# Another order of a hybrid-layer step: planner costs, sample search and first feed-forward units

## Chip, cores and metric

The kernel runs on one core of a Trainium2 chip. The metric is the device time of one execution in microseconds (us). Of the engines, TensorE (PE) multiplies, VectorE (DVE), ScalarE (ACT) and GpSimd (POOL) work elementwise, and SyncE (SP) issues most DMAs.

## What is computed

One step of one decoder layer, for a prompt of 1024 tokens and for 64 sample tokens (8 sequences of 8, each with 4096 past positions in a paged cache). The two token mixers run on the same input; cut to what matters here:

```python
def select_keys(scores, q_pos, topk):            # topk = 256
    scores = jnp.where(admissible, scores, -jnp.inf)
    _, idx = lax.top_k(scores, topk)
...
def token_mixer(x, ...):
    z = split_projection(x @ w_in)
    attn = attend(q_a, k_a, v_a, q_i, k_i, z['w_i'])     # softmax over the selected keys
    log_a = jax.nn.log_sigmoid(z['a_b'] @ w_alpha2 + b_alpha) / GATE_TAU
    o_b, s_new = gla_chunked(q_b, k_b, v_b, log_a, s0, chunk)   # 4 heads, chunks of 64
    o_b = rms_norm(o_b) * gla_norm_g * jax.nn.silu(z['g_b'])
    merged = jax.nn.sigmoid(z['gate_a']) * (attn @ w_attn_o) + jax.nn.sigmoid(z['gate_b']) * (o_b @ w_gla_o)
    return merged @ w_out, ...
...
def residual_block(x, mix_out, ...):
    h = layer_norm(DN_ALPHA * x + mix_out, ln1_g, ln1_b)
    ff = jnp.square(jax.nn.relu(h @ w_ff1)) @ w_ff2      # 1024 -> 4096 -> 1024
    return layer_norm(DN_ALPHA * h + ff, ln2_g, ln2_b)
```

## The kernel before

The 1088 tokens lie on the free axis in three chunks of 384, 384 and 320 columns (the third holds the sample tokens), and features on the partitions. Every large product is done three times with operands split in a high and a low part (`xh`·`wh`, `xl`·`wh`, `xh`·`wl`); a weight tile is loaded as `wr`, ACT rounds it to `wh`, and DVE or POOL subtracts to get `wl` (`sub` picks the one that the planner's clock has free first; in the feed-forward part the tiles are `w`).

Nothing schedules itself on the chip: every engine runs its instructions in the order of the program. That order is made by a planner in Python. `Clock` holds a time for each engine, adds a cost for each instruction (`cost`), and knows when each tile is ready. Work is written as generators (`Stream`), which yield the tiles that they need next. `Order.run` takes the first stream in its list whose needs are ready by PE's time plus 0.2, and records its next piece; where none is, the one that is ready soonest. Each stream has a `slack` (how far it may run ahead of DVE and ACT) and a `margin`. All recording goes through one line (223), so that the profile shows that line everywhere, and the rows are told apart by tiles.

In the first half (`front`) the streams are, among others:
- `top_prompt`: the threshold of the 256 largest index scores of each prompt token, found bit by bit in 32 rounds; DVE counts (`jk`) in two groups of tiles (`ga`, `gb`), each with small steps `_m`, `_u`, `_f`. Its masks `msk` are needed by the attention.
- `top_sample`: the same for the sample tokens, with the counts on ACT (`jka`, two per round), a small product that sums pairs of partitions on PE (`ppr`), and small steps on DVE (`gs_m`, `gs_u`, `gs_f`), 33 rounds in all. It may start at job `merge_at + SEARCH`.
- `heads`: the four heads of the gated linear attention. For head h, DVE scans the log gates (`cu`), multiplies `gk` by their exponential, and then PE starts with `psas` from `gq` and `gk`.
- `main`: the projections as a list of jobs, among them 16 `gate` jobs that serve as filler, `pmb` (o_b @ w_gla_o), `pma` (attn @ w_attn_o) and `pwo` (merged @ w_out).
- `at_soft` and `at_pv`: prompt attention: scores `psq`, masked `pp`, transpose `ppt`, split `phl`, values `pov`. It starts when the heads and `top_prompt` are done.
- `ob_load`: loads the gated output of the heads back from DRAM as `obl` and splits it into `obh` and `obl` for `pmb`. It may start three jobs ahead of the merge when the last `pov` is done, and else with the merge.

In the second half (`back`) the norms (`ln`: products `plm`, `plv`, `plr`, tiles `h`) feed the feed-forward units (`ff1_unit`: product `pf`, relu, square, split into `a`), with the attention of the sample tokens between (`psc`, `pob`, `sa`, `pso`).

Of the kernel before, what the change touches and what calls it, by code (L numbers as in the profile page):

```python
# [17 lines left out]
AF = mybir.ActivationFunctionType  # L18
# [5 lines left out]
P = 128  # L24
# [11 lines left out]
CH = ((0, 384), (384, 384), (768, 320))  # L36
# [9 lines left out]
NBW = 5  # L46
NCW = 8
NSM = 6
NSH = 6
# [9 lines left out]
GAHEAD = 2  # L59
BLEAD = 1  # L60
MARGIN = 0.0
DMAL = 2.75
LAG = 0.3
LAGS = {"pe": 0.2}
POOLLAG = 0.4
M_IP = 0.0
M_IS = 0.0
M_TS = 0.3
SEARCH = -22
M_GL = 0.0  # L70
# [3 lines left out]
M_SC = 1.0  # L74
M_SD = 0.5
WLATE = 4.0

# [5 lines left out]
def view(ap, offset, dims):  # L83
    return bass.AP(tensor=ap.tensor, offset=ap.offset + offset, ap=[list(d) for d in dims])


class Clock:
# [3 lines left out]
    def __init__(self, uses):  # L91
        self.uses, self.left, self.seen, self.key = uses, {}, {}, {}
        self.free, self.owed, self.short = {}, {}, []
        self.t = dict.fromkeys(("pe", "dve", "act", "pool", "sp"), 0.0)
        self.ring = {}
        self.fly = deque(maxlen=8)
        self.written = {}
        self.used = {}
        self.after = {}
        self.banks = [None] * 8  # L100
        self.psum = set()
        self.pinned = set()
# [58 lines left out]
    def cost(self, e, op, outs, ins):  # L161
        n = outs[0].free_size() if callable(outs[0].free_size) else outs[0].free_size
        aps = len(outs) + len(ins)
        if e == "pe":
            dt = ins[-1].dtype
            f = 4 if dt == F32 and op != "transpose" or dt == F32R and n < 256 else 1
            return max(f * n / 2400 + 0.0135, 0.11)
        if e == "dve":
            return 0.069 + n * (0.00625 if op == "reciprocal" else 0.00104) + 0.06 * (aps > 3)
        if e == "act" and "dma" in op:  # L170
            return 0.06
        if e == "act":
            return (0.051 if any(x.tensor.name in self.psum for x in ins) else 0.093) + n / 1200 + 0.093 * (aps - 2)
        if e == "pool":
            if "dma" in op:
                return 1.25
            if op == "tensor_scalar":
                return 0.26 + 0.00333 * n
            return 0.13 + n * 0.0009 if op in ("affine_select", "memset") else 0.15 + n * 0.0021
        return 0.52 if hasattr(outs[0].tensor, "tag") else 0.7  # L180

    def note(self, e, op, a, k):
# [9 lines left out]
        if e == "sp" and len(self.fly) == 8:  # L192
            self.t[e] = max(self.t[e], self.fly[0])
        start = max([self.t[e]] + [self.ready(x) for x in ins] + [self.after.get(x.tensor.name, 0.0) for x in outs])
        self.t[e] = end = start + self.cost(e, op, outs, ins)
        if "dma" in op:
# [93 lines left out]
def hybrid_step(ctx, tc, A, O, uses):  # L290
# [43 lines left out]
    with ExitStack() as ph:  # L334
        back(ph, tc, env, A, O)
    return {k: n for k, n in clock.seen.items() if k[1] is not None}


def front(ph, tc, env, A, O):
# [1108 lines left out]
    for h in range(4):  # L1448
# [8 lines left out]
    more_gates(4)  # L1457
    for j in range(2):
# [58 lines left out]
    mix_at = len(jobs)  # L1517
    env["deep"] = mix_at - 2
    env["alone"] = (merge_at,)
# [112 lines left out]
    s_gl = order.add(heads(), margin=M_GL)  # L1632
    s_ts = order.add(top_sample(), slack=1.0, margin=M_TS)
    s_main = order.add(main(), engines=())
# [8 lines left out]
def back(ph, tc, env, A, O):  # L1643
# [114 lines left out]
    def ln(c, z, s, gi, emit, tag):  # L1758
# [46 lines left out]
        normed.add((tag, c))  # L1805

    def add(s, z, f):

# [18 lines left out]
    def outputs(c, get, make):  # L1827
# [10 lines left out]
        for f in range(8):  # L1838
# [11 lines left out]
            if f < 7 or c < 2:  # L1850
                add(s[:, :n], z, f)
        order.add(ln(c, z, s[:, :n], 0, emit_h(c), 1), at=0)

# [3 lines left out]
    def project():  # L1857
# [4 lines left out]
        for f in range(8):  # L1862
# [3 lines left out]
            mg[f, 1] = (st[:, 0], st[:, 1])  # L1866
        order.add(ln(0, zs, env["rsum"], 0, emit_h(0), 1), at=0)
        yield from outputs(1, lambda f: W.get(f, 2, NRW), page)
# [248 lines left out]


    def ff1_unit(w, f, c, a):
        n = CH[c][1]  # L2120
        ps = bank("pf1", True)
        yield from mm3(ps[:, :n], w, [hc[k, c] for k in range(8)])
        unpin(ps)
        r = small("fr")
        act.activation(r[:, :n], ps[:, :n], AF.Relu)
# [59 lines left out]
    def feed():  # L2185
        for i0, (cc, k0, np_) in zip(first, plan):
            a, z, s = {}, {c: [] for c in cc}, {}
            if k0 == 0:
                ws = {}
                for c in cc:  # L2190
                    yield lambda: (1, c) in normed
                    for f in range(np_ + 8):
# [20 lines left out]
            for f in range(8):  # L2213
                w = W.get(i0 + np_ + f, *((2, NRW) if cc == (2,) else ()))
                for c in cc:
                    n = CH[c][1]
                    z[c].append((yield from ff2_unit(w, f, c, a, np_, False)))
                    if k0 + np_ == 32:
# [4 lines left out]
                        if f == 7:  # L2223
                            order.add(ln(c, z[c], s[c][:, :n], 2, emit_y(c), 2), at=0)

# [60 lines left out]
def build(arrays, uses):  # L2286
    nc = bacc.Bacc("TRN2", target_bir_lowering=False, num_devices=1, dynamic_dma_scratch_size=SCRATCH)
    A = {k: nc.dram_tensor(k, v.shape, mybir.dt.from_np(v.dtype), kind="ExternalInput").ap() for k, v in arrays.items()}
    O = {k: nc.dram_tensor(k, s, F32, kind="ExternalOutput").ap() for k, s in OUT.items()}
    with tile.TileContext(nc) as tc:  # L2290
        return nc, hybrid_step(tc, A, O, uses)

# [20 lines left out]
```

## Time and profile before

| | us |
|---|---|
| median of 3 runs | 2145.94 (2145.61 to 2147.4) |
| profiled execution | 2150.88 |
| its span (first to last instruction) | 2149.2 |
| PE busy | 2061.4 (96%) |
| weight loads of PE busy | 1965.4 (91%) |
| DVE busy | 1347.3 (63%) |
| ACT busy | 1030.8 (48%) |
| POOL busy | 717.0 (33%) |

The span is the time between the first and the last instruction of the profiled execution. The granted TensorE clock is 0.983 of full on the mean. A row of waits says which engine's instruction waited for which other one's; a wait for several is put down to the one that came last.

### The profile page before, as it was taken

What the parts mean: (1) busy time and instruction counts of PE and PEld (TensorE: products, weight loads), DVE (VectorE), ACT (ScalarE), POOL (GpSimd) and SP (SyncE); (2) the same over time, 40 slices, a digit from 0 to 9 for tenths busy, and PEclk for the clock granted to TensorE, in tenths of its full rate; (3) what the DMA queues carried; (4) which work ended last, traced back from release to release, by engine and by line L of the source; (5) the groups of instructions that cost most, each with busy time, mean ns of one, the idle gap of its engine ahead of it and who ended that gap; (6) DMA issues with size and microseconds to landing.
All of it is one profiled execution on the core that took longest, in us unless ns stands there. A gap on an engine that the chain in (4) does not pass through costs nothing.

```text
span 2149.2 us, 34662 instructions
## 1 busy us (share of the span) xinstructions
PE 2061.4 (96%) x12492; PEld 1965.4 (91%) x12507; DVE 1347.3 (63%) x2806; ACT 1030.8 (48%) x2010; POOL 717.0 (33%) x543
## 2 busy tenths in 40 slices
PE   7999988998999999998999999999999999999997
PEld 7978977897989999998998999989999999999996
DVE  7887998898236666532656854665654446367635
ACT  5665234444667667776133424445453333245543
POOL 5144211215121121231334335545544333343342
PEclk9999998999999999999999999999999999999998
DMA  9363401211213242344393224545433442145442
GB/s 334 150 181 109 143 29 42 64 59 48 75 48 126 72 128 71 93 174 143 129 344 112 79 76 118 163 126 157 142 94 113 147 134 72 61 129 169 169 148 83
DMA packets 182860, 260.79 MB, mean 121 GB/s; under 512 B 21392, under 2 KB 118672, under 8 KB 182688
## 3 DMA queue, kind: packets, MB, share of 16 engines
q1 hardware_dynamic: 175136, 233.14, 33.4%
q0 software_dynamic: 7552, 25.43, 3.7%
q8 instruction: 98, 1.61, 0.3%
q14 instruction: 74, 0.61, 0.1%
HBM read 209.00 MB, written 49.51 MB: 120 GB/s over the span
## 4 chain that ended last, share of the span: by engine, by line
PE 69%; DVE 17%; issue 5%; ACT 4%; DMA 2%; POOL 2%; SPq 0%; DVEq 0%; ACTq 0%; POOLq 0%
PE pf L223 30%; PE gate L223 8%; DVE jk L223 5%; PE pwo L223 3%; PE psc L223 2%; PE psv L223 2%; PE po L223 2%; PE pmb L223 2%; PE gb L223 2%; PE qi L223 1%; PE pob L223 1%; PE psq L223 1%; PE pov L223 1%; PE ppt L223 1%; PE psi L223 1%
## 5 line engine op out<-in xcount | busy, mean ns | idle before, releaser
L223 PE MATMUL pf<-a,w 128*128 128x384 f32 (+1 forms) x2304 | 401.7, 330 | 3.9 <-ACT a L223 1.9
L223 PE MATMUL pf<-h,w 128*128 128x384 f32 (+1 forms) x2304 | 396.2, 329 | 2.2 <-DVE h L223 2.2
L223 PEld LDWEIGHTS pf<-a,w 128*128 128x128 f32 x2304 | 380.3, 189 | 6.4 <-ACT a L223 2.5
L223 PEld LDWEIGHTS pf<-h,w 128*128 128x128 f32 x2304 | 380.2, 189 | 4.8 <-DVE h L223 3.1
L223 POOL TENSOR_TENSOR wl<-wr,wh 128x1024 fp32r<-128x1024 f32 (+1 forms) x68 | 156.1, 2300 | 546.4 <-ACT wh L223 450.3
L223 DVE TENSOR_TENSOR w<-wr,w 128x512 fp32r<-128x512 f32 x190 | 178.8, 966 | 74.0 <-ACT w L223 72.6
L223 ACT ACTIVATE w<-wr 128x512 fp32r<-128x512 f32 x272 | 156.8, 619 | 49.1 <-PE pf L223 26.4
L223 POOL TENSOR_TENSOR a<-fr,a 128x384 fp32r<-128x384 f32 (+1 forms) x79 | 76.0, 963 | 275.1 <-ACT a L223 267.5
L223 POOL TENSOR_TENSOR w<-wr,w 128x512 fp32r<-128x512 f32 x82 | 113.0, 1390 | 81.7 <-ACT w L223 76.0
L223 PE MATMUL gate<-xh,wh 128*128 128x384 f32 (+1 forms) x384 | 130.2, 339 | 0.0
L223 DVE TENSOR_TENSOR acc<-acc,pf 128x384 f32<-128x384 f32 (+1 forms) x136 | 72.5, 538 | 87.1 <-PE pf L223 85.1
L223 PE MATMUL gate<-xl,wh 128*128 128x384 f32 (+1 forms) x384 | 126.1, 328 | 0.0
L223 PE MATMUL gate<-xh,wl 128*128 128x384 f32 (+1 forms) x384 | 126.0, 328 | 0.0
L223 ACT ACTIVATE fr<-pf 128x384 f32<-128x384 f32 (+1 forms) x96 | 45.1, 470 | 154.2 <-PE pf L223 153.5
L223 DVE TENSOR_TENSOR fr<-fr,pf 128x384 f32<-128x384 f32 (+1 forms) x96 | 50.8, 529 | 101.7 <-ACT fr L223 100.6
L223 ACT ACTIVATE wh<-wr 128x1024 fp32r<-128x1024 f32 (+1 forms) x75 | 74.4, 1006 | 56.6 <-PE pmb L223 35.2
L223 ACT ACTIVATE a<-fr 128x384 fp32r<-128x384 f32 (+1 forms) x96 | 48.8, 508 | 95.1 <-DVE fr L223 93.9
L223 DVE TENSOR_SCALAR_CACHE_REDUCE jk<-sc,gb_f 128x896 int8<-128x896 f32 (+2 forms) x96 | 92.7, 966 | 1.1
L223 DVE TENSOR_SCALAR_CACHE_REDUCE jk<-sc,ga_f 128x1024 int8<-128x1024 f32 (+2 forms) x96 | 88.4, 921 | 1.0
L223 PE MATMUL psv<-wh,xh 128*128 128x256 f32 (+1 forms) x288 | 83.0, 288 | 0.0
L223 PE MATMUL psv<-wh,xl 128*128 128x256 f32 (+1 forms) x288 | 81.3, 282 | 0.0
L223 PE MATMUL psv<-wl,xh 128*128 128x256 f32 (+1 forms) x288 | 81.3, 282 | 0.0
(460 smaller groups left out, 5116.7 us busy)
## 6 DMA issues: line engine op xcount, KB each, us to landing
wr<-wff SPq DMA_DIRECT2D x256, 256.0 KB
wr<-w SPq DMA_DIRECT2D x43, 512.0 KB
ckr<-kT SPq DMA_DIRECT2D x256, 64.0 KB
ga_s<-gate SPq DMA_DIRECT2D x16, 544.0 KB
ci_s<-cig SPq DMA_DIRECT2D x16, 512.0 KB
kir<-ci_s SPq DMA_DIRECT2D x16, 512.0 KB
wr<-wout SPq DMA_DIRECT2D x13, 512.0 KB
mgp<-ga_s SPq DMA_DIRECT2D x16, 384.0 KB
```

What stands on the lines that cost most here:

```text
L223: r = f(*a, **k)
```

## The change

It has three parts.

The planner's numbers: `Clock` now keeps the last spans of DVE and POOL that use the port which the two share (`locks`), and starts an instruction of one behind such a span of the other; it adds 1.28 where ACT's function table changes; a scan costs 0.0021 per element instead of 0.00104, a POOL instruction 0.175 + 0.0022 n instead of 0.15 + 0.0021 n, and the 40% that were added to a POOL result's readiness (`POOLLAG`) are dropped.

The sample search: it may start eight jobs earlier (`SEARCH` −22 to −30), with a slack of 3.0 instead of 1.0 and a margin of 0.2 instead of 0.3.

The back: a norm is put into the list of streams behind the norms that are still under way, not ahead of them. The first four feed-forward units of a chunk, which waited for the whole norm (`(1, c) in normed`), are computed by `ff1_first`: for each of the first six k-tiles, as the norm emits it, the products of all four units, then the last two k-tiles unit by unit. (The `Counted` exception ends a first counting pass early and leaves the instructions alone; `NGATE` and `DEEP` name numbers that were there.)

```diff
-POOLLAG = 0.4
+POOLLAG = 0.0
-M_TS = 0.3
-SEARCH = -22
+M_TS = 0.2
+SEARCH = -30
...
+    def locks(self, e, op, outs, ins):
+        n = outs[0].free_size() if callable(outs[0].free_size) else outs[0].free_size
+        if e == "pool":
+            return "dma" not in op and op not in ("iota", "memset")
+        if any(x.tensor.name in self.psum for x in outs + ins if (x.size() if callable(x.size) else x.size) > P) or len(outs) > 1:
+            return False
+        return op not in ("memset", "reciprocal", "tensor_tensor_scan", "tensor_reduce") and (op != "tensor_scalar" or n > 1)
...
+        held = e in self.shared and self.locks(e, op, outs, ins)
+        if held:
+            for lo, hi in self.shared["pool" if e == "dve" else "dve"]:
+                if lo <= start < hi:
+                    start = hi
...
-    s_ts = order.add(top_sample(), slack=1.0, margin=M_TS)
+    s_ts = order.add(top_sample(), slack=TS_SLACK, margin=M_TS)
...
+        norms.append(order.add(ln(*a), at=sum(not x.done for x in norms)))
...
-        order.add(ln(c, z, s[:, :n], 0, emit_h(c), 1), at=0)
+        norm(c, z, s[:, :n], 0, emit_h(c), 1)
...
+    def ff1_first(ws, c, a):
+        n = CH[c][1]
+        ps = [bank("pf1", True) for _ in ws]
+        for ks in [[k] for k in range(KFIRST)] + [list(range(KFIRST, 8))]:
+            for f, w in enumerate(ws):
+                for k in ks:
+                    if f == 0 or len(ks) > 1:
+                        yield lambda: (k, c) in hc
+                        yield [hc[k, c][1]]
+                    h, l = hc[k, c]
+                    pe.matmul(ps[f][:, :n], w[0][k], h, start=k == 0, stop=False)
+                    pe.matmul(ps[f][:, :n], w[0][k], l, start=False, stop=False)
+                    pe.matmul(ps[f][:, :n], w[1][k], h, start=False, stop=k == 7)
+                if ks[-1] == 7:
+                    unpin(ps[f])
+                    ff1_out(ps[f], f, c, a)
+                yield ()
...
-                    yield lambda: (1, c) in normed
...
-                        if f < np_:
+                        if f < np_ == 4:
+                            w4 = [w] if f == 0 else w4 + [w]
+                            if f == 3:
+                                yield from ff1_first(w4, c, a)
```

The number of PE instructions is the same, 12258; on DVE there are 31 fewer, on POOL 33 more. What moves is the order, and the order decides three places.

On DVE, ahead of `gk` of GLA head 0 (the first number is the row's place in the engine's order; `jk` are counts of the prompt search, `cu` the scanned gates). Before:

```order
444 L223 TENSOR_SCALAR ga_f_1460<-ga_u_1459 128x3
445 L223 TENSOR_SCALAR jk_263,ga_n_1462<-sc7_409,ga_f_1460 128x1024
446 L223 TENSOR_SCALAR gb_m_1468<-gb_n_1469 128x3
447 L223 TENSOR_SCALAR jk_263,ga_n_1462<-sc4_412,ga_f_1460 128x640
448 L223 COPY_PREDICATED gb_u_1466<-gb_m_1468,gb_f_1467 128x3
449 L223 TENSOR_SCALAR jk_263,ga_n_1462<-sc4_412,ga_f_1460 128x384
450 L223 TENSOR_SCALAR gb_f_1467<-gb_u_1466 128x3
451 L223 TENSOR_SCALAR jk_263,gb_n_1469<-sc6_410,gb_f_1467 128x896
452 L223 TENSOR_SCALAR ga_m_1461<-ga_n_1462 128x3
453 L223 TENSOR_SCALAR jk_263,gb_n_1469<-sc5_411,gb_f_1467 128x768
454 L223 COPY_PREDICATED ga_u_1459<-ga_m_1461,ga_f_1460 128x3
455 L223 TENSOR_TENSOR gk0_2708<-gk0_2708,cu_3114 128x1088
```

Now:

```order
414 L254 TENSOR_TENSOR gsc0_3233<-cu_3092 128x8
415 L254 TENSOR_TENSOR cu_3092<-cu_3092,gmd_3234 128x1024
416 L254 TENSOR_SCALAR jk_263,gb_n_1665<-sc6_409,gb_f_1663 128x896
417 L254 TENSOR_SCALAR ga_m_1657<-ga_n_1658 128x3
418 L254 TENSOR_SCALAR jk_263,gb_n_1665<-sc5_410,gb_f_1663 128x768
419 L254 COPY_PREDICATED ga_u_1655<-ga_m_1657,ga_f_1656 128x3
420 L254 TENSOR_SCALAR jk_263,gb_n_1665<-sc3_412,gb_f_1663 128x512
421 L254 TENSOR_SCALAR ga_f_1656<-ga_u_1655 128x3
422 L254 TENSOR_TENSOR gk0_2690<-gk0_2690,cu_3092 128x1088
423 L254 TENSOR_SCALAR jk_263,ga_n_1658<-sc7_408,ga_f_1656 128x1024
```

The step on `ga_f` that stood in the middle of the search rows ahead of head 0's `cu` now stands right ahead of `gk0`, which comes 33 rows earlier on its engine. On PE, `psas` of that head goes from row 1661 to 1691.

On PE, around the last scores `psq` of the attention. Before, the last gate jobs follow them (numbers 12 to 17):

```order
L223 MATMUL gate11_2_9440<-xh6_122,wl40_0_8973 128x320
L223 MATMUL gate11_2_9440<-xh7_123,wh40_0_8972 128x320
L223 MATMUL gate11_2_9440<-xl7_131,wh40_0_8972 128x320
L223 MATMUL gate11_2_9440<-xh7_123,wl40_0_8973 128x320
L223 MATMUL ppt_9502<-idf_95,pp_9347 128x128 x4
L223 MATMUL gate12_0_9526<-xh0_116,wh41_0_9264 128x384
L223 MATMUL gate12_0_9526<-xl0_124,wh41_0_9264 128x384
```

Now the last gate (17) ends ahead of them, and `pmb` follows the attention directly:

```order
L254 MATMUL gate17_2_10113<-xh7_123,wl46_0_9628 128x320
L254 MATMUL psq_10225<-kar10_8622,qq03_10060 128x128
L254 MATMUL psq_10225<-kar11_8623,qq03_10060 128x128
L254 MATMUL pov_10138<-phl_10151,vpr1_8624 128x256 x4
L254 MATMUL ppt_10241<-idf_95,pp_10062 128x128 x4
L254 MATMUL pov_10240<-phl_10246,vpr1_8624 128x256 x4
L254 MATMUL ppt_10274<-idf_95,pp_10139 128x128 x2
L254 MATMUL pov_10273<-phl_10277,vpr1_8624 128x256 x2
L254 MATMUL ppt_10295<-idf_95,pp_10177 128x128 x2
L254 MATMUL pov_10294<-phl_10298,vpr1_8624 128x256 x2
L254 MATMUL pmb_10344<-obh0_10307,wh47_0_9918 128x384
```

The gate jobs, which lay in part behind the attention, are used up ahead of its end.

On SP's queue, the first loads of `obl`. Before, they stand behind the store of gate 14:

```order
L223 DMA wr45_0_9781<-w1 128x1024
L223 DMA ga_s4_90<-gate14_9787 128x1088
L223 DMA wr46_0_9881<-w1 128x1024
L223 DMA obl0_9895<-ob_s0_75 128x384
L223 DMA obl1_9896<-ob_s1_76 128x384
```

Now, behind the store of gate 17:

```order
L254 DMA at_s1_84<-ahl_10099 64x2x128 x2
L254 DMA ga_s7_93<-gate17_9922 128x1088
L254 DMA mgt_10193<-ga_s0_86 128x1088
L254 DMA mgt_10195<-ga_s1_87 128x1088
L254 DMA obl0_10197<-ob_s0_75 128x384
L254 DMA obl1_10198<-ob_s1_76 128x384
```

The loads went three gates back in the gates' order. The 34 `ppr` pairs of the sample search stand between PE's rows 2809 and 5373 before, and between 1977 and 4205 now.

## Rows read from the trace of the kernel before

**Rows 1.** Busy time, share of the span and instructions of each engine.

```profile
PE 2061.4 (96%) x12492; PEld 1965.4 (91%) x12507; DVE 1347.3 (63%) x2806; ACT 1030.8 (48%) x2010; POOL 717.0 (33%) x543
```

**Rows 2.** Waits of PE: who waited for whom, us in total, times, longest us.

```profile
PE psas L223 <- DVE gk L223: 26.0, 3, 16.4
...
PE ppr L223 <- ACT jka L223: 6.4, 4, 2.3
PE po L223 <- DVE rl L223: 5.6, 3, 5.1
...
PE pso L223 <- DVE sa L223: 3.6, 1, 3.6
PE pf L223 <- DVE h L223: 2.2, 3, 1.3
```

**Rows 3.** Timeline of PE: start us, us, engine, operation, [idle before it, releaser].

```profile
329.51 0.44 PE L223 MATMUL psas<-gq,gk 128*64 128x64 f32 x2 [16.44 <-DVE gk L223]
...
405.74 0.45 PE L223 MATMUL psas<-gq,gk 128*64 128x64 f32 x2 [2.98 <-DVE gk L223]
...
518.31 0.45 PE L223 MATMUL psas<-gq,gk 128*64 128x64 f32 x2 [6.62 <-DVE gk L223]
```

**Rows 4.** Windows: us, each engine's busy us (instructions), PEclk, DMA share, GB/s.

```profile
135.40:138.90 3.50, 3.36 (x8) 2.25 (x9) 0.93 (x3) 0.60 (x1) 0.00 (x0) 0.51 0.99 295
329.50:333.50 4.00, 3.99 (x19) 3.88 (x20) 3.93 (x14) 1.46 (x3) 0.78 (x2) 0.52 0.00 0
405.70:412.00 6.30, 6.26 (x25) 6.17 (x26) 6.15 (x16) 1.44 (x3) 2.57 (x3) 0.51 0.55 165
518.30:524.60 6.30, 6.29 (x27) 6.09 (x28) 6.15 (x10) 1.73 (x4) 2.86 (x3) 0.51 0.38 114
1423.50:1429.20 5.70, 5.68 (x19) 5.03 (x20) 4.00 (x13) 1.75 (x3) 0.00 (x0) 0.51 0.23 69
124.00:535.00 411.00, 379.07 (x2262) 342.18 (x2261) 365.51 (x817) 175.03 (x346) 120.32 (x58) 0.95 0.27 85
299.62:328.08 28.46, 13.45 (x83) 13.19 (x82) 28.09 (x59) 7.37 (x13) 8.25 (x4) 0.79 0.18 55
917.00:983.00 66.00, 63.80 (x386) 63.48 (x385) 23.56 (x48) 47.09 (x88) 21.90 (x14) 0.97 0.44 156
1430.00:2130.00 700.00, 696.44 (x4341) 683.53 (x4348) 376.43 (x624) 291.42 (x553) 288.85 (x249) 1.00 0.40 127
```

**Rows 5.** Timeline of DVE, columns as in rows 3.

```profile
127.00 1.26 DVE L223 TENSOR_SCALAR_CACHE_REDUCE jk<-sc,ga_f 128x1024 int8<-128x1024 f32 x1
...
299.45 0.17 DVE L223 TENSOR_SCALAR ga_f<-ga_u 128x3 int32<-128x3 int32 x1
...
317.48 1.79 DVE L223 COPY_PREDICATED ga_u<-ga_m,ga_f 128x3 int32<-128x3 int32 x1
...
328.08 1.28 DVE L223 TENSOR_TENSOR gk<-gk,cu 128x1088 f32<-128x1088 f32 x1
...
1416.13 5.52 DVE L223 CAST aqz<-aq 64x32 fp32r<-64x32 f32 x8 [1.24 <-POOL aqz L223]
```

**Rows 6.** Window of DVE, instructions on tile jk alone.

```profile
299.62:328.08 28.46, 16.33 (x34) 0.79 0.18 55
```

**Rows 7.** Waits of DVE, columns as in rows 2.

```profile
DVE gs_m L223 <- PE ppr L223: 79.0, 25, 5.9
```

**Rows 8.** Timeline of SyncE, ACT, DVE at the loads and splits of obl.

```profile
943.59 9.13 SPq L223 DMA_DIRECT2D obl<-ob_s  x16
...
951.10 0.51 ACT L223 ACTIVATE obh<-obl 128x384 fp32r<-128x384 f32 x1
...
963.55 7.34 DVE L223 TENSOR_TENSOR obl<-obl,obh 128x384 fp32r<-128x384 f32 x6 [0.27 <-ACT obh L223]
```

**Rows 9.** Timeline of POOL beside the DVE steps of rows 5.

```profile
316.89 4.66 POOL L223 TENSOR_TENSOR wl<-wr,wh 128x1024 fp32r<-128x1024 f32 x2 [24.14 <-ACT wh L223]
```

**Rows 10.** Costliest groups: operation, count | busy us, mean ns | idle before, releaser.

```profile
L223 POOL TENSOR_TENSOR w<-wr,w 128x512 fp32r<-128x512 f32 x82 | 113.0, 1390 | 81.7 <-ACT w L223 76.0
```

More of the change, by code (lines that the diff above doesn't have):

```diff
@@ L47 @@
 NCW = 8
+KFIRST = 6
 NSM = 6
@@ L60 @@
 BLEAD = 1
+DEEP = 2
+TS_SLACK = 3.0
 MARGIN = 0.0
@@ L75 @@
 M_SD = 0.5
+NGATE = 4
 WLATE = 4.0
@@ L84, in view @@
     return bass.AP(tensor=ap.tensor, offset=ap.offset + offset, ap=[list(d) for d in dims])
+class Counted(Exception):
+    pass
 class Clock:
@@ L99, in __init__ @@
         self.after = {}
+        self.shared = {"dve": deque(maxlen=24), "pool": deque(maxlen=8)}
+        self.table = 0
         self.banks = [None] * 8
@@ L168, in cost @@
         if e == "dve":
-            return 0.069 + n * (0.00625 if op == "reciprocal" else 0.00104) + 0.06 * (aps > 3)
+            return 0.069 + n * {"reciprocal": 0.00625, "tensor_tensor_scan": 0.0021}.get(op, 0.00104) + 0.06 * (aps > 3)
         if e == "act" and "dma" in op:
@@ L178, in cost @@
                 return 0.26 + 0.00333 * n
-            return 0.13 + n * 0.0009 if op in ("affine_select", "memset") else 0.15 + n * 0.0021
+            return 0.13 + n * 0.0009 if op in ("affine_select", "memset") else 0.175 + n * 0.0022
         return 0.52 if hasattr(outs[0].tensor, "tag") else 0.7
+    def locks(self, e, op, outs, ins):
[5 more added lines that the diff above has]
+        return op not in ("memset", "reciprocal", "tensor_tensor_scan", "tensor_reduce") and (op != "tensor_scalar" or n > 1)
     def note(self, e, op, a, k):
@@ L194, in note @@
         start = max([self.t[e]] + [self.ready(x) for x in ins] + [self.after.get(x.tensor.name, 0.0) for x in outs])
+        held = e in self.shared and self.locks(e, op, outs, ins)
[3 more added lines that the diff above has]
+                    start = hi
+        if e == "act" and "dma" not in op:
+            f = {AF.Ln: 1, AF.Sqrt: 2, AF.Exp: 0, AF.Tanh: 0}.get(a[2] if len(a) > 2 else k.get("func"), self.table)
+            if f != self.table:
+                self.table = f
+                start += 1.28
         self.t[e] = end = start + self.cost(e, op, outs, ins)
+        if held:
+            self.shared[e].append((start, end))
         if "dma" in op:
@@ L335, in hybrid_step @@
         back(ph, tc, env, A, O)
-    return {k: n for k, n in clock.seen.items() if k[1] is not None}
+    seen = {k: n for k, n in clock.seen.items() if k[1] is not None}
+    if not uses:
+        raise Counted(seen)
+    return seen
 def front(ph, tc, env, A, O):
@@ L1456, in front @@
                 job(wtile(19 + 2 * (h - 1) + j), g_job(h - 1, j), lambda h=h: "o" in G[h - 1])
-    more_gates(4)
+    more_gates(NGATE)
     for j in range(2):
@@ L1517, in front @@
     mix_at = len(jobs)
-    env["deep"] = mix_at - 2
+    env["deep"] = mix_at - DEEP
     env["alone"] = (merge_at,)
@@ L1805, in ln, with norm @@
         normed.add((tag, c))
+    norms = []
+    def norm(*a):
+        norms.append(order.add(ln(*a), at=sum(not x.done for x in norms)))
     def add(s, z, f):
@@ L1866, in project @@
             mg[f, 1] = (st[:, 0], st[:, 1])
-        order.add(ln(0, zs, env["rsum"], 0, emit_h(0), 1), at=0)
+        norm(0, zs, env["rsum"], 0, emit_h(0), 1)
         yield from outputs(1, lambda f: W.get(f, 2, NRW), page)
@@ L2123, in ff1_unit, with ff1_out @@
         unpin(ps)
+        ff1_out(ps, f, c, a)
+    def ff1_out(ps, f, c, a):
+        n = CH[c][1]
         r = small("fr")
@@ L2223, in feed @@
                         if f == 7:
-                            order.add(ln(c, z[c], s[c][:, :n], 2, emit_y(c), 2), at=0)
+                            norm(c, z[c], s[c][:, :n], 2, emit_y(c), 2)
     def main():
@@ L2289, in build @@
     O = {k: nc.dram_tensor(k, s, F32, kind="ExternalOutput").ap() for k, s in OUT.items()}
-    with tile.TileContext(nc) as tc:
-        return nc, hybrid_step(tc, A, O, uses)
+    try:
+        with tile.TileContext(nc) as tc:
+            return nc, hybrid_step(tc, A, O, uses)
+    except Counted as c:
+        return None, c.args[0]
 def kernel(**inputs):
```

3 lines of the change are left out of this document (added).

## The prediction

> **What bounds the kernel now.** I began with the page's busy times: TensorE (PE) is at work 96% of the span, VectorE (DVE) 63% [rows 1]. PE is the bound, and with the same 12258 PE instructions in both programs, time is to be had only where PE stands idle or runs at half clock. PE's waits say where: 26.0 us in three waits for `gk` from DVE, then 6.4 for `jka`, 5.6 for `rl`, 3.6 for `sa`, 2.2 for `h` [rows 2]. PE's timeline gives the places of the three: 16.44, 2.98 and 6.62 us ahead of the first `psas` product of GLA heads 0, 1 and 2 [rows 3]. The windows then show what an idle stretch leaves behind: right after these waits the granted clock is 0.52 for 4.0 us and 0.51 for 6.3, that is the lower of its two levels (1.2 GHz); the third wait is followed by 6.3 us at 0.51 again [rows 4].
>
> Why is `gk` late? In 124 to 535 us DVE is busy 365.51 of 411 us, almost as much as PE with 379.07 [rows 4]: it counts for the prompt's top-256 search (`jk`, `ga`, `gb`) in the same queue as the GLA preparation. Between the search step at 299.45 and `gk` at 328.08 [rows 5] DVE worked 28.09 of 28.46 us [rows 4], 16.33 of it in counts alone [rows 6], while PE had nothing to do after 313.07 (329.51 less 16.44). So head 0 isn't late because its own chain is long; search rows stand ahead of it.
>
> **The change, part by part.** The device work is nearly the same; the planner now reckons other durations and so writes another order. What counts is the order.
>
> *GLA heads (gain).* In the new DVE order the search row that ran at 299.45 is the last one ahead of head 0's `gk`. What ran between it and `gk` in before was 28.09 us; 16.33 us are counts and about 5 the small steps between them, and these 21 us go behind `gk`, while the rest, GLA's own chain, stays. On PE 30 matmuls more stand ahead of `psas`; at 0.16 us, the mean of 4341 in 696.44 us [rows 4], and less for these narrower ones, that is 4 us. Against the 16.4 us of wait 21 + 4 − 16.4 = 9 us would be in hand, less the 7 us by which PE comes earlier through the `rl` term below: 2 us, the thinnest margin of the sum. For heads 1 and 2 I added up the durations in the same way: `gk` moves forward on DVE by 22.5 and 46 us, its `psas` back on PE by 19 and 7 us. Against the waits, and less what PE then comes earlier by (25 and 31 us), 14 and 16 us stay in hand. So all 26.0 us should go. With them goes the low clock behind them: 4.0 us at 0.52 and twice 6.3 at 0.51 cost 1.9 + 3.1 + 3.1 = 8.1. Term: **−34** (bounds −18, if only head 0's goes with its clock, and −34).
>
> *`rl` at 130 us (gain).* PE waited 5.13 us for it; two search counts (the first of 1.26 us [rows 5]) stood ahead of it on DVE. In the new order no count does, and 24 matmuls of `va`, 4 us, stand on PE between the scores and the product that takes `rl`; 1.3 + 4 is more than 5.1. −5.1, and 3.5 us at 0.51 behind it [rows 4], −1.7: **−7** (0 to −7).
>
> *Sample search (gain, with a risk).* It has 33 rounds, each two `jka` counts on ScalarE (ACT), a `ppr` pair on PE, small steps on DVE. In before most of them ran among the last gates and the first `pmb`, where PE waited for `jka`: 6.4 us [rows 2]. In the new order the first pair stands at PE row 1977 and the last at 4205 (2809 and 5373 before), far ahead of the attention's end, with other matmuls between all of them. **−6** (0 to −6). The cost is on DVE, which after each round has `gs_m` waiting for `ppr`: 79.0 us in 25 waits in before [rows 7], 3.2 each, with the rows queued behind held as well. That was a stretch in which DVE had little else; now 19 rounds fall ahead of head 3's `psas`. I take 0, because the orders leave 41 us in hand there by the same sums and the planner lets `ppr` end first; the rival below prices it.
>
> *`sa` at 1420 us (gain).* PE waited for `sa`, which stood behind eight small casts of 5.52 us on DVE [rows 5]. They now stand behind it. −3.6, and half of 5.7 us at 0.51 [rows 4]: **−6** (0 to −6).
>
> *First feed-forward units (gain).* Four units now run k-tile by k-tile as the norm emits them, so that 12 matmuls stand between two tiles of `h`. The 2.2 us for `h` go, at most; the wait for the norm's mean ahead of it (1 to 2 us) stays. **−2** (+3 to −4).
>
> *Attention's end (loss).* By the new order the prompt's mask comes later against PE (first `psq` at PE row 3463 instead of 3324, filled with gates), so the 16 gate jobs run out with the attention instead of after it. In before 66 us of gates lay between the last attention product and `pmb` (917 to 983 us [rows 4]). They hid two things. First the loads of `obl`: 16 DMAs on SyncE's queue, from 943.59, first split by ACT at 951.10, last split on DVE ending at 963.55 + 7.34 = 970.9 [rows 8]. In the new order they stand behind the store of the last gate, so they start about when PE ends `gate17_2`. Left on PE are then 22 attention products, 3 us, and `pmb`, which needs all splits of a chunk. The first split comes 7.5 us after the first issue, so PE can't begin before about 9 us after `gate17_2` (7.5 and 1.5 for ACT's sigmoid and the issues ahead) and loses 6 us; `pmb` then follows at the pace of the splits. From the last load to the last split 27 us passed in before; the 72 matmuls of `pmb` that use these chunks take 12. If the splits keep that pace, PE loses 27 + 1.5 − 3 − 12 = 13.5. Second, the last softmax steps, whose chain lies inside the same idle time. **+14**, the low clock behind included (6 to 20).
>
> *Reshuffle.* 49 weight splits `w` move from DVE to GpSimd (POOL), 21 of `a` back. In 1430 to 2130 us PE is busy 696.44 of 700, DVE 376.43, POOL 288.85 [rows 4]; there is room. The attention stage, with 11 sample rounds in it, will have some new short waits. **+3** (0 to 12).
>
> Sum: −34 − 7 − 6 − 6 − 2 + 14 + 3 = −38. The profiled execution took 2150.88 us (span 2149.2), which gives 2112.9; it lies 4.9 above the median of the runs, so the forecast is **2108**.
>
> **One rule weighed.** Row first: while POOL split two 128x1024 weights (4.66 us from 316.89 [rows 9]), a DVE step on three elements a partition took 1.79 us, beginning at 317.48; a like step took 0.17 at 299.45 [rows 5]. The Trainium skill, SBUF — State Buffer, section "Who interferes with whom", says that the two engines share a port pair as an exclusive lock, so that the one that issues second waits for the whole instruction; the trace agrees. The Trainium skill, Perfetto Trace Analysis, section "Optimizing Scalar/DVE Operations", draws from it that handing work from one to the other might not help, which speaks against the 49 splits moved. The rival that follows from it is the third below.
>
> **Rivals.**
> 1. *The waits go only in part.* DVE is 89% busy in 124 to 535 us, and 2 us in hand at head 0 is little. If heads 1 and 2 keep their waits with their clock (2.98 + 6.62 + 6.2) and `rl` stays (7), 23 us less are gained: **2131**. For it: the thin margin. Against: the order itself, in which the search rows are no longer ahead.
> 2. *The sample rounds hold up DVE (slower).* 19 rounds ahead of head 3, each holding DVE for `ppr`. At 2.2 us each the 41 us in hand are used up; at the 3.2 mean, 61 us, PE comes 20 us late: 2128. At 5.9, the longest [rows 7], it is 112 − 41 = 71 late: 2179. It is slower than before from (41 + 38) / 19 = 4.2 us per round; a likely time then is **2160**. For it: PE's queue is now never idle, so `ppr` waits for its place. Against: in before DVE waited because it had nothing else queued.
> 3. *POOL and DVE hold each other up in the feed-forward part.* A `w` split is 1390 ns on POOL [rows 10], so 49 × 1.39 = 68 us of POOL more, in which DVE may be held; if a quarter is felt by PE, 17 us: **2125**. Against: PE's waits for POOL in the whole run are single microseconds.
> 4. *The end of the attention is hidden after all*, by attention products that the ACT chain delays less than the order suggests, and the norm gains fully: −14 and −4: **2090**.
> 5. *The order doesn't matter much*, the stalls reappear next door: within 4 us of **2146**.
>
> **How the numbers follow.** Forecast (2100 to 2118) 0.45; rival 1 0.17; rival 4 0.13; rival 3 0.07; rival 5 0.05; rival 2 0.13, of which 0.05 stays below 2141. A measurement of this kernel tells about 0.2% (4 us) from no change. Faster: 0.45 + 0.17 + 0.13 + 0.07 + 0.05 = 0.87; same 0.05; slower 0.08. The range leaves out the slow half of rival 2, rival 5 and the far side of rival 4: **2086 to 2136**.
>
> **What would show it.** PE's waits without `psas<-gk` and `po<-rl` (right); a new wait `pmb<-obh` or `obl` of 8 to 14 us between the last `pov` and the first `pmb` (right); DVE's wait for `ppr` under 2.2 us each ahead of 535 us. Wrong, if `psas` still waits over 5 us, or if new waits for `pp`, `phl` or `msk` over 15 us in all stand in the attention.

## The result and the profile after

The changed kernel takes **2122.4 us** (median of 4 runs, 2120.89 to 2123.98) against 2145.78 on the same chip: ratio 0.9891 with a 95% interval of 0.9874 to 0.9908, 23.4 us faster. The forecast was 2108 within 2086 to 2136. Its profiled execution took 2120.89 us, the lowest of the four, so that the two profiles lie 30.0 us apart and the medians 23.4.

Busy times (columns as in [rows 1]) and the line of the granted clock in 40 slices of the span:

```profile
PE 2052.5 (97%) x12507; PEld 1958.7 (92%) x12507; DVE 1316.4 (62%) x2775; ACT 1024.7 (48%) x2008; POOL 776.2 (37%) x576
...
PEclk9999999999999999998999999999999999999998
```

PE's waits, which answer to [rows 2]:

```profile
PE pov L254 <- ACT phl L254: 17.5, 3, 14.8
...
PE psi L254 <- DVE qi L254: 6.5, 1, 6.5
PE pwo L254 <- DVE mg L254: 3.9, 3, 2.9
PE pf L254 <- POOL w L254: 1.8, 1, 1.8
PE psc L254 <- DVE aqz L254: 1.5, 1, 1.5
...
PE po L254 <- DVE rl L254: 1.0, 1, 1.0
...
PE pso L254 <- DVE sa L254: 0.7, 1, 0.7
```

No wait for `gk` is left, none for `jka`, and 1.0 us for `rl`. New on top is `phl` with 17.5 us. The windows (columns as in [rows 4]) show the same: from the first gate product of the GLA heads to the first attention scores, 287 to 654 us, PE is busy for the whole 367.00 us at full clock, while at the attention's end 23.9 us run at 0.50 with PE at work for 8.62 of them.

```profile
287.00:654.00 367.00, 367.00 (x2270) 332.08 (x2270) 273.87 (x674) 228.26 (x479) 93.52 (x53) 1.00 0.21 69
943.30:967.20 23.90, 8.62 (x25) 7.35 (x26) 8.42 (x12) 9.07 (x23) 7.30 (x7) 0.50 0.66 237
```

To see where the 30 us lie, I took for each matmul the time to the start of the next, less the lower quartile of that time for its shape, and summed it by stage. It counts idle time and low clock together, in both profiles over all matmuls:

| stage, from its first product | before | after |
|---|---|---|
| `psi` (index scores) | 5.2 | 8.5 |
| `pss` | 10.1 | 4.0 |
| `psa` (GLA heads) | 76.9 | 43.5 |
| `psq` (attention) | 7.3 | 5.5 |
| last 200 matmuls ahead of `pmb`, and `pmb` | 13.5 | 26.5 |
| `pwo` | 7.3 | 7.1 |
| first units, `pf` | 9.0 | 10.6 |
| sample attention to the end | 35.6 | 29.1 |

The reckoning also counts products that merely run longer than the quartile of their shape (the heads after have 43.5 us, though PE is busy there throughout at the full clock), so only the differences tell. The heads give 33.4 us and `pss` 6.1. The attention's end takes back 13, and that although the waits for `jka` left this stage (6.4 us [rows 2], 8 with the low clock behind them as an estimate): its new loss is 20 to 21 us.

**What happens there.** ACT's timeline in the changed kernel (start, length, instruction, idle before it and releaser):

```profile
942.74 0.39 ACT L254 ACTIVATE phl<-ppt 128x256 fp32r<-128x256 f32 x1
957.17 0.42 ACT L254 ACTIVATE ahl<-ao 64x256 fp32r<-64x256 f32 x1 [14.04 <-DMA at_s<-ahl]
...
959.03 0.38 ACT L254 ACTIVATE phl<-ppt 128x256 fp32r<-128x256 f32 x1
...
959.72 0.92 ACT L254 ACTIVATE obh<-obl 128x384 fp32r<-128x384 f32 x2
```

and SyncE's queue:

```profile
939.01 0.34 SPq L254 DMA_DIRECT2D ga_s<-gate  x1
...
940.77 9.02 SPq L254 DMA_DIRECT2D obl<-ob_s  x16
950.39 17.45 SPq L254 DMA_DIRECT2D at_s<-ahl  x12
```

ACT stands still for 14.04 us ahead of an `ahl`, the tile in which the attention's output is split. It has two buffers, and the next is free only when its store `at_s<-ahl` has landed. These stores stand on SyncE behind the 16 `obl` loads (9.02 us of issues) and are issued from 950.39 on; ACT goes on at 957.17. SyncE's own waits between 938 and 970 us show what paces these issues:

```profile
SPq L254 <- DMA obl<-ob_s: 3.0, 12, 0.6
```

The transfers issued by SyncE and ACT take turns with eight semaphores (counters that tell when a transfer has landed), and none of the 837 issues for which the trace has both times comes before the transfer issued eight earlier has landed. The ninth load is issued at 945.81, when the first has landed at 945.79, and the first store at 950.39, when the ninth load has landed at 950.38. The first four stores then land between 956.9 and 957.4, just behind the last load (956.7). The `phl` at 959.03, which PE's `pov` needs, stands behind that `ahl` in ACT's queue, and so do all splits of `obl`, the first at 959.72, though the loads began at 940.77. PE's wait is 14.8 us.

**The new wait in `psi`.** DVE's timeline and SyncE's queue:

```profile
72.00 0.17 DVE L254 TENSOR_SCALAR gn<-gn 128x2 f32<-128x2 f32 x1 [13.11 <-DMA gn<-gla_norm_g]
72.21 2.17 DVE L254 TENSOR_TENSOR qi<-qi,qi 64x320 fp32r<-64x320 f32 x4
```

```profile
40.77 22.18 SPq L254 DMA_DIRECT2D ci_s<-cig  x8
...
64.40 0.74 SPq L254 DMA_DIRECT2D gn<-gla_norm_g  x1
```

DVE waits 13.11 us for a load of two columns, `gn`. On SyncE that load now stands behind eleven stores of gathered index pages, the last eight of them in these 22.18 us; before, it stood behind six of the sixteen and was issued at 41.12. The `qi` splits wait behind it on DVE, and PE 6.5 us for them.

### The profile page after: what moved, and what is told of

It reads as the page before. It is cut to its first block, busy times and chain, and to the rows that moved or that the text cites. A ratio compares the mean times of both kernels' runs of the same rounds, so it can differ in the third digit from the quotient of the medians.

```text
span 2119.2 us, 34591 instructions
## 1 busy us (share of the span) xinstructions
PE 2052.5 (97%) x12507; PEld 1958.7 (92%) x12507; DVE 1316.4 (62%) x2775; ACT 1024.7 (48%) x2008; POOL 776.2 (37%) x576
## 4 chain that ended last, share of the span: by engine, by line
PE 88%; DVE 3%; issue 3%; DMA 3%; POOL 1%; ACT 1%; SPq 0%; ACTq 0%; DVEq 0%; POOLq 0%
PE pf L254 33%; PE gate L254 9%; PE psv L254 5%; PE gb L254 5%; PE pwo L254 4%; PE pmb L254 4%; PE psc L254 3%; PE po L254 3%; PE qb L254 2%; PE kb L254 2%; PE qa L254 2%; PE pma L254 2%; PE qi L254 2%; PE psq L254 2%; PE pov L254 1%
## 5 line engine op out<-in xcount | busy, mean ns | idle before, releaser
L254 POOL TENSOR_TENSOR w<-wr,w 128x512 fp32r<-128x512 f32 x131 | 187.3, 1437 | 134.9 <-ACT w L254 121.9
L254 DVE TENSOR_TENSOR w<-wr,w 128x512 fp32r<-128x512 f32 x141 | 147.1, 1052 | 54.8 <-ACT w L254 50.7
L254 POOL TENSOR_TENSOR a<-fr,a 128x384 fp32r<-128x384 f32 (+1 forms) x58 | 56.9, 980 | 202.0 <-ACT a L254 202.0
```

The source lines that it names most:

```text
L254: r = f(*a, **k)
```

## The experiments

All ratios are against the kernel before on the same chip, with 95% intervals.

| run | ratio | interval |
|---|---|---|
| changed kernel | 0.9891 | 0.9874 to 0.9908 |
| x1 four `ahl` buffers | 0.9867 | 0.9843 to 0.9890 |
| x2 early `obl` loads | 0.9836 | 0.9820 to 0.9853 |
| x3 search as before | 0.9972 | 0.9959 to 0.9985 |
| x4 search alone | 0.9955 | 0.9941 to 0.9969 |
| y1 back alone | 1.0046 | 1.0029 to 1.0063 |
| y2 front alone | 0.9879 | 0.9863 to 0.9896 |
| y3 early `gn` load | 0.9871 | 0.9853 to 0.9889 |
| y4 early `obl` and `gn` | 0.9821 | 0.9804 to 0.9837 |
| z1 stores by ACT | 0.9888 | 0.9869 to 0.9907 |
| z2 port not counted | 0.9908 | 0.9892 to 0.9925 |
| z3 norms' place alone | 1.0018 | 1.0008 to 1.0028 |
| z4 y4, stores by ACT, no `ff1_first` | 0.9868 | 0.9850 to 0.9887 |

**x1: what holds ACT.**

```diff
-            hl = cs[0].tile([P, 256], F32R, name="ahl", tag="ahl", bufs=2)
+            hl = cs[0].tile([P, 256], F32R, name="ahl", tag="ahl", bufs=4)
```

> The changed kernel with four buffers for the tile ahl in place of two; nothing else moves in the order. Theory: at the attention's end ACT stands still because its next ahl tile is held by a store that is queued on SyncE behind the 16 obl loads, and phl stands behind that in ACT's queue. Then PE's wait for phl falls from 14.8 us to under 4, ACT begins the obl splits as the loads land (near 950 us instead of 959.7), and the time is 2110 to 2117. Rival (the forecast's own mechanism): what holds PE is the arrival and splitting of obl; then the wait only changes its name, to pmb, and the time stays at 2120 to 2124.

Measured 2117.9 us, 0.9867. ACT's timeline, then PE's waits:

```profile
944.20 1.05 ACT L254 ACTIVATE obh<-obl 128x384 fp32r<-128x384 f32 x2
955.56 0.42 ACT L254 ACTIVATE ahl<-ao 64x256 fp32r<-64x256 f32 x1 [10.31 <-DMA at_s<-ahl]
```

```profile
PE pmb L254 <- ACT obh L254: 8.6, 1, 8.6
...
PE pov L254 <- ACT phl L254: 3.5, 3, 1.5
```

With two buffers more, ACT gets two `ahl` further before it stands still, 10.31 us until a store has landed. The wait for `phl` is down to 3.5 us, and two `obl` splits come at 944.20. But the held `ahl` now stands between the splits, and PE waits 8.6 us for `obh`. So the store behind the loads is what holds ACT; what waits on PE's side is whatever stands next in ACT's queue. The signs of the theory came (`phl` under 4 us, early splits), and so did the rival's change of name to `pmb`. The stage still loses 22.8 us by the reckoning above, and a fall in time isn't clear from the interval.

**x2 and y4: the loads earlier.**

```diff
-NPV = 32
+NPV = 24
```

> The changed kernel, but the obl loads may start when 24 of the 32 attention units are done (NPV 24 for 32), so that they stand some gates earlier on SyncE. Theory that the loads' place on SyncE's queue costs the 20 us at the attention's end, by whichever wait: nearly all of it comes back, 2102 to 2108. Rival: the attention's own chain through ACT, without gates beside it, sets its end; then 2115 to 2122.

Measured 2114.7 us against 2149.8 before on this chip, 0.9836: 0.55% better than the changed kernel's ratio, some 12 us, of the 20 that the theory wanted. In y4 the four small loads were also moved ahead on SyncE (y3 alone is below):

> Early obl loads (NPV 24) and the early small loads together on the changed kernel. Theory that both waits are independent: about 0.981 of before (0.979 to 0.983), below the early loads alone (0.9836). Rival, that what PE gains at 70 us is lost again at head 0, where little is in hand: waits for gk of 3 us or more and 0.983 to 0.985.

Measured 2110.2 us, **0.9821**, the fastest kernel of the study, though not clear of x2. The time is the theory's; the rival's wait for `gk` came too, for a reason that is shown below at y3. PE's waits:

```profile
PE psas L254 <- DVE gk L254: 3.1, 1, 3.1
...
PE pov L254 <- ACT phl L254: 3.2, 3, 1.2
...
PE ppt L254 <- ACT pp L254: 2.7, 3, 1.4
```

No wait for `phl` of more than single microseconds is left, yet the stage still loses 20.4 us by the reckoning above (20.5 in x2). They are short waits of the softmax chain, for `phl`, `pp`, `wl`, and the low clock between them. So of the 26.5 us that the changed kernel loses, the loads' place is worth about 6; for the rest the rival of x2 is right. Gates to fill these gaps are used up. x4 and z2 (below) have 264 and 174 gate products behind the last scores `psq` and lose 0.5 and 0.6 us in this stage, 14 and 8 with the attention ahead of it; the changed kernel has none there and loses 26.5 and 32.

**x3 and x4: costs or search?**

```diff
-SEARCH = -30
+SEARCH = -22
```

> The changed kernel with the sample search let in where it was before (SEARCH -22 for -30), slack and margin as changed. Theory that the planner's new costs alone took the waits for gk away: psas waits for gk stay under 2 us in all, and the time is 2105 to 2125. Rival, that the early search made room on DVE: 15 us or more of these waits come back and the time is above 2130.

Measured 2143.1 us, 0.9972. There is no wait for `gk` at all, so the early search isn't what freed head 0. But the time was missed by 18 us and more. PE's waits:

```profile
PE pov L254 <- ACT phl L254: 10.1, 7, 2.8
...
PE ppt L254 <- ACT pp L254: 8.4, 3, 6.4
...
PE pov L254 <- DVE phl L254: 4.2, 10, 1.0
```

The sample rounds now run beside the attention, ACT has their counts to do, and `phl` and `pp` come late in 20 short waits: the last stage loses 47.1 us. What the heads gave is given back there.

The other way round, the kernel before with the search's three numbers alone:

> The kernel before with the three numbers of the sample search alone (start, slack, margin). Theory that the planner's costs took the waits for gk away: they stay near 26 us here, the ppr waits go (7 us), and the obl loads fall behind the last gate all the same, which costs 15 to 20 us: 2150 to 2162, slower than before. Rival, that the search made the gain: waits for gk under 5 us and 2118 to 2130.

Measured 2140.5 us, 0.9955. PE's waits:

```profile
PE psas L223 <- DVE gk L223: 16.4, 1, 16.4
...
PE po L223 <- DVE rl L223: 5.8, 3, 5.1
...
PE ppr L223 <- ACT jka L223: 2.8, 3, 1.2
```

Head 0 waits 16.4 us as before, which speaks for the costs again. The waits for heads 1 and 2 went, which I hadn't expected, but the heads as a stage lose no less than before, to within 1 us: PE now waits there for `gs_m` (3.8 us) and `jka` (2.8) of the sample rounds, and for `Sm` (2.5) on ACT. The loss at the attention's end went too (0.5 us in that stage), while the attention ahead of it loses some 5 us more: with the early search, and without the time gained at the heads, gates are left for the end. So my expectation of a slower kernel was wrong.

**z2: which cost?**

```diff
-        held = e in self.shared and self.locks(e, op, outs, ins)
+        held = False
```

> The changed kernel, but the planner doesn't count the port that DVE and POOL share; the other costs stay. In its order gk of head 0 stands at DVE row 438 (422 in the changed kernel, 455 before) and its psas at PE row 1673 (1691, 1661). Theory that the moved search rows ahead of gk take the waits away: about half of the 16 rows' 14 us stay, so that PE waits 5 to 11 us for gk at head 0, and the time is 5 to 15 us above the changed kernel's (0.991 to 0.996 of before). Rival, that the scan's and the tables' costs do it and the port counts for nothing: under 3 us for gk, 0.987 to 0.990.

Measured 2126.9 us, 0.9908. PE's wait:

```profile
PE psas L254 <- DVE gk L254: 14.3, 1, 14.3
```

Without the port in the plan head 0 waits 14.3 us (more than I had worked out), heads 1 and 2 not at all. Counting the port is what brings `gk` of head 0 forward. It is worth 14 us there and yet only about 4 in the whole (0.9908 against 0.9891, intervals that overlap), because this kernel loses 0.6 us at the attention's end and the changed one 26.5. The port's counting is also what saves time from the sample attention to the end: z2 loses some 37 us in that stage. The nine kernels planned with the port lose 28 to 30 there, the five planned without it 35 to 40.

**y1, y2 and z3: the back.**

> The kernel before with the back's part alone: the place of the norms in the list of streams and ff1_first; the front's order is as before. Theory, from the two traces: the wait for h at the first units stays (2.2 us before, 2.7 after), some 2 us are lost there and 4 us are gained where the last norms come in the order of the chunks: 2 to 6 us faster than before, 0.997 to 0.999. Rival, the forecast's own term: the h wait goes, which alone would be 2 to 4 us. PE's wait for h in the profile tells them apart: above 2 us by the theory, under 1 by the rival.

Measured 2159.0 us, 1.0046: slower by 10 us, against both. PE's timeline at the first units:

```profile
1198.26 0.79 PE L254 MATMUL pf<-h,w 128*128 128x384 f32 x3 [1.22 <-DVE w L254]
1201.35 1.65 PE L254 MATMUL pf<-h,w 128*128 128x384 f32 x4 [2.29 <-DVE w L254]
```

The wait for `h` is gone, as in the rival, and 3.5 us of waits for weights `w` stand there: four units at once want four units' weights where one was wanted. The 2.7 us that the expectation took for `h` after the change were waits for `w` too (0.9 us on ACT, 1.8 on POOL); the changed kernel's list has none for `h`.

> The kernel before with the planner's costs and the search's numbers, without the back's part. Theory that the whole gain is the front's: 17 to 23 us faster than before (0.989 to 0.992), PE's waits at the attention's end as in the changed kernel (14 to 16 us for phl). Rival, that the back carries a good part of it: less than 14 us faster.

Measured 2123.3 us, 0.9879: the front alone is as fast as the whole change, within the intervals.

> The kernel before with the new place of the norms in the list of streams alone, without ff1_first; six rows of PE's order differ, all at the last norms. Theory that ff1_first made the back alone slower (it wants four units' weights where one was wanted): here 0.997 to 1.001. Rival, that the place of the norms did it: 1.003 or more.

Measured 2150.4 us, 1.0018: between theory and rival. The new place of the norms alone costs some 4 us (the stage to the end loses 39.5 for 35.6), `ff1_first` some 6 more in the old front. In the new front no run shows harm by either: y2 without them and the changed kernel with them agree within the intervals, and z4, which leaves `ff1_first` out, loses 5 us less at the first units and 4 us more in the stage ahead of them.

**y3: the load of `gn`.** The edit moves four DMA issues ahead of `def later()`:

```diff
+    sp.dma_start(wa2[64:80, :], A["wa2"])
+    sp.dma_start(b_al, A["b_alpha"])
+    sp.dma_start(gn5, A["gla_norm_g"])
+    sp.dma_start(env["lnp"], A["ln"])
     def later():
```

> The changed kernel with the four small loads (wa, b_alpha, gla_norm_g, ln) issued on SyncE ahead of the gathered index pages' stores, not behind eight of them. Theory: DVE's step on gn, which stood 13.1 us at 72.0 us for its load, held the qi splits behind it, and PE waited 6.5 us in psi for these; without it the psi wait is under 3 us and the time 3 to 6 us below the changed kernel's, 0.987 to 0.988 of before. Rival: DVE has room there, PE waits in psi for something else: the same time within 2 us.

Measured 2122.8 us, 0.9871, not clear of the changed kernel. The `psi` stage loses 0.5 us instead of 8.5, but 3 of these 8 us are lost ahead of it instead. PE doesn't wait for `qi` in y3, y4 and z4, which have the early load, and does for 1.8 to 6.5 us in the six kernels with the changed order there and the late one; so the late load is the likely cause, though the planner also moves some `psi` products and `qi` splits in these three. The changed kernel's 6.5 is the longest of the six. At head 0 PE waits again:

```profile
PE psas L254 <- DVE gk L254: 3.1, 1, 3.1
```

The same 3.12 us stand in x2, y2, y4 and z1, but not in the changed kernel, x1 and z4. The orders of PE, DVE, ACT and POOL are the same up to there in the changed kernel, x1, x2, y2 and z1; y3, y4 and z4 differ from them in `psi` only. So it isn't the order, nor PE's coming earlier: in x1 and z1 PE gets there at 311.4 and 311.1 us. DVE's and POOL's timelines of y3 around `gk`:

```profile
308.30 2.08 DVE L254 TENSOR_SCALAR ga_f<-ga_u 128x3 int32<-128x3 int32 x1
310.30 1.28 DVE L254 TENSOR_TENSOR gk<-gk,cu 128x1088 f32<-128x1088 f32 x1
```

```profile
308.01 2.35 POOL L254 TENSOR_TENSOR wl<-wr,wh 128x1024 fp32r<-128x1024 f32 x1 [0.32 <-POOL gq L254]
310.32 2.27 POOL L254 TENSOR_TENSOR gqz<-gq,bcol 128x512 f32<-128x512 f32 x1
```

and those of the changed kernel, with ACT's:

```profile
311.27 0.16 DVE L254 TENSOR_SCALAR ga_f<-ga_u 128x3 int32<-128x3 int32 x1
311.34 1.28 DVE L254 TENSOR_TENSOR gk<-gk,cu 128x1088 f32<-128x1088 f32 x1
```

```profile
311.35 1.05 ACT L254 ACTIVATE wh<-wr 128x1024 fp32r<-128x1024 f32 x1
...
312.53 2.37 POOL L254 TENSOR_TENSOR wl<-wr,wh 128x1024 fp32r<-128x1024 f32 x1 [1.87 <-issue]
314.86 1.17 POOL L254 TENSOR_TENSOR gqz<-gq,bcol 128x512 f32<-128x512 f32 x1
```

In y3 a POOL split `wl` starts at 308.01, and DVE's step on three elements, `ga_f`, which comes 0.29 us behind, takes 2.08 us, as long as the split; `gk` comes behind it. In the changed kernel `ga_f` takes 0.16: it starts 1.26 us ahead of the split, which has to wait for ACT's `wh` (to 312.40), not for DVE. The other direction stands one row further: POOL's `gqz` takes 2.27 us in y3, where `gk` began 0.02 us ahead of it, and 1.17 in the changed kernel, where `gk` is over. Which of the two issues first decides, as the Trainium skill has it (SBUF — State Buffer, section "Who interferes with whom"); the trace agrees in both directions.

What tips it lies some 50 us ahead of `gk`. Counted from the first `psa` product, the three executions without the wait run alike to a few hundredths of a microsecond by then, and so do the five with it. The fork stands where both engines meet at an earlier split. In the changed kernel:

```profile
247.84 1.06 ACT L254 ACTIVATE wh<-wr 128x1024 fp32r<-128x1024 f32 x1
...
260.44 0.17 DVE L254 TENSOR_SCALAR ga_f<-ga_u 128x3 int32<-128x3 int32 x1
...
260.77 2.40 POOL L254 TENSOR_TENSOR wl<-wr,wh 128x1024 fp32r<-128x1024 f32 x1 [7.03 <-ACT wh L254]
```

and in x2:

```profile
250.24 1.06 ACT L254 ACTIVATE wh<-wr 128x1024 fp32r<-128x1024 f32 x1 [0.31 <-DMA wr<-wvb]
...
262.81 2.40 POOL L254 TENSOR_TENSOR wl<-wr,wh 128x1024 fp32r<-128x1024 f32 x1 [6.69 <-ACT wh L254]
...
262.83 2.41 DVE L254 TENSOR_SCALAR ga_f<-ga_u 128x3 int32<-128x3 int32 x1
```

DVE is 0.33 us ahead of POOL in the one and 0.02 behind in the other, and stays 1.4 us or more later from there to `gk`. The difference comes from ACT's split 13 us earlier. In the five executions with the wait, ACT stood 0.3 to 0.7 us for a weight that had not landed; POOL's next split came later by that, and DVE's step `ga_m` beside it was held for 1.80 to 2.14 us. In the other three it was 1.37 to 1.44. So some tenths of a microsecond in the landing of one load are behind the 3.1 us at head 0.

**z1 and z4: the stores on another queue.**

```diff
-                sp.dma_start(view(f32(at_s[c]), ...
+                (act if "obl" in flags else sp).dma_start(view(f32(at_s[c]), ...
```

> The changed kernel, but the attention output's stores that are recorded after the obl loads are issued by ACT, not by SyncE; the loads stay where they are. Theory: the stores behind the loads on SyncE's queue are what held ahl and with it ACT; then no wait for phl or obh above 3 us stands at the attention's end, the splits follow the loads, and 8 to 12 us of the changed kernel's time come back (0.984 to 0.986 of before). Rival: the stores are slow because the DMA engines are full with the loads, whoever issues them; then ACT waits for ahl for 6 us or more all the same and the time changes by less than 3 us (0.988 or more).

Measured 2121.3 us, 0.9888: no gain, as the rival had it. ACT's timeline:

```profile
951.25 1.64 ACTq L254 DMA_DIRECT2D at_s<-ahl  x2
952.93 0.38 ACT L254 ACTIVATE ao<-pov 64x256 f32<-64x256 f32 x1 [7.87 <-DMA obl<-ob_s]
```

ACT's own store is issued at 951.25 only, and the next instruction has waited 7.87 us, until a load of `obl` had landed. A store that another engine issues while the loads run is no quicker. The trace's semaphores show what holds the issue: ACT waits for the semaphore that its store will use, and the load of `obl` that used it before landed at 951.17. So it is the order that the program sets between its transfers: the eight semaphores are shared by both engines' queues. Once issued, this store took 4.9 us more to land (956.17); between 850 and 935 us in the changed kernel the median was 2.1.

> The changed kernel with the early obl loads, the early small loads, the attention's later stores issued by ACT, and the first units unit by unit as before (no ff1_first). Theory that these waits add up: 0.978 to 0.981 of before. Rival, that PE then arrives too early at head 0 and at the attention's last softmax steps: 0.982 or more.

Measured 2117.4 us, 0.9868, worse than y4. The stores by ACT do the same harm again, 8.36 us:

```profile
924.41 1.47 ACTq L254 DMA_DIRECT2D at_s<-ahl  x2
925.93 0.38 ACT L254 ACTIVATE ao<-pov 64x256 f32<-64x256 f32 x1 [8.36 <-DMA obl<-ob_s]
```

and without `ff1_first` PE waits 3.7 us for the norm's sums. The rival named other places, so neither was right on the cause; the stores should have stayed on SyncE.

## Why the prediction was right, and where its steps failed

The measured 2122.4 us lie in the stated range, but outside the 2100 to 2118 to which the forecast itself gave 0.45. The mechanism was right at the heads and in part wrong at the attention's end, and there the prediction's own sign of being wrong came: new waits for `phl` of 17.5 us, over the 15 that it allowed. Its sign of being right, a wait of 8 to 14 us for `obh` or `obl` ahead of the first `pmb`, didn't (0.5 us). That the time is in the range owes something to the range's width.

- **GLA heads: right, in place and size.** −34 forecast, 33.4 us in the stage. The size holds for executions without a wait at head 0, as the profiled one; in the five others the stage loses 4 to 6 us more, so that some 28 are gained. The margin was thinner than the 2 us forecast: `gk` ends at 312.62 and `psas` starts at 313.06. Where one POOL split gets the port ahead of DVE, 2 us long, 3.1 us of wait appear. z2 shows that the port's counting moved this `gk`, x3 that the search's start didn't.
- **`rl`: right.** −7 forecast; the stage gives 6.1.
- **Sample search: right on both sides.** The waits for `jka` (6.4) are gone, and the rival in which DVE is held by the rounds didn't come: 7.7 us in 5 waits (79.0 in 25 before, [rows 7]), far under the 2.2 us a round that were in hand. Ahead of 535 us there is one of them, of 0.8 us.

```profile
DVE gs_m L254 <- PE ppr L254: 7.7, 5, 3.1
```

- **`sa`: mis-sized.** −6 forecast. The wait fell from 3.6 to 0.7, but the small casts that were moved behind it now hold `psc` for 1.5 us, and the low clock comes with that.
- **First units: wrong in sign or nothing.** −2 forecast; the stage loses 10.6 us where it lost 9.0. The wait moved from `h` to `w`, which the step hadn't looked for.
- **Attention's end: right in place, mis-sized, other mechanism.** +14 forecast with bounds of 6 to 20; 20 to 21 measured. That the gates run out was right. I had followed the loads into `pmb`, as a question of when splits come. I took the 7.5 us of before from the first issue to the first split; it is 19.0 us now (940.77 to 959.72), because I hadn't followed what stands behind the loads on SyncE: stores that free a tile on ACT. (The 27 us of that step run from the first issue, not from the last load.) The larger error is the second thing that the gates hid, the last softmax steps. I put them inside the same idle time, at nothing of their own; with the loads early (x2, y4) the stage still loses 20 us to them.
- **Not in the sum:** `psi`, +3.3, the same kind of error at another place, a small load that fell behind stores on SyncE (the size varies: 6.2 to 8.5 us in six executions with this order, 5.1 to 5.2 in three with that of before and 0.4 in a fourth, z3); and −6.5 between the sample attention and the end, of which `sa` is only a part. The planner's new split of work between DVE and POOL stands there in y2, without the back's part, too (27.7), and not in z2, so it comes with the port's counting; which of its moves gives it stays open.
- **From profile to median.** I took 4.9 us off, as the kernel before showed. The changed kernel's profiled execution lies 1.5 below its median, and single executions of one kernel differ by up to 11 us (x2: 2112.2 to 2123.1), so that step can't be more exact than some microseconds.
- **Rivals.** The one on DVE and POOL (2125) came nearest in time, nearer than the forecast, and not for its reason: the stage where it was to show got faster. The slower side didn't come; x3 shows what would have made it: sample rounds that fall into the attention, on ACT rather than DVE.

## What to carry to other kernels

When idle time is taken out of a full engine, ask what it was that filled the gaps further on: here the gate products now run out ahead of the attention's end, and more than half of the gain at the heads is lost there. For a transfer that moves on a queue, look not only at who waits for it, but at what it is now ahead of: a store that frees a buffer holds its engine, and everything queued behind on that engine, whatever that is needed for. Here the missing fill was worth some 20 us of the stage's 26.5 and the held store some 6; the longest wait in the list named only the second. And a part of a change that looks like a gain by itself (units tile by tile of the norm) may want its inputs earlier than anything gives them.

## What the hardware showed that I had not expected

A store issued behind 16 loads let its tile go only 6.8 us after the first issue (950.39 to 957.17), and a store issued by ACT in that time came no sooner (7.87 and 8.36 us of standing in z1 and z4): every issue waits there until an earlier transfer with the same one of eight semaphores has landed, whichever engine issues. Nor had I expected that one and the same order has two outcomes at the port of DVE and POOL: 2.08 us or 0.16 for a step on three elements, and with it 3.1 us of PE's wait or none, by whether a weight had landed some tenths of a microsecond sooner. The one profiled execution of x2 has this wait and is its slowest (2123.1 us); how much of the 11 us to its fastest is due to it isn't shown, as the others weren't profiled.
